# TensorE's order in two mixer branches, written out by a small planner instead of left to the scheduler

## The chip, the cores and the metric

The kernel runs on one core of a Trainium2 chip. The metric is the device time of one execution in microseconds (us), taken as the median of several runs. The engines in the rows are PE (TensorE, matmuls and transposes), DVE (VectorE), ACT (ScalarE), POOL (GpSimd), and SP, which here only issues DMAs.

## The reference

One decoder layer over 512 positions of width 1024, in float32. The part that matters:

```
h    = rmsnorm(x);  q,k,v,o,i,f | q,k,v | gates = split(h @ w_in)
A    = mlstm(silu(conv4(q)), silu(conv4(k)), v, i, f)          # 4 heads of 128
ya   = (sigmoid(o) * head_rmsnorm(A)) @ w_br_m
a    = softmax(q1 k1' / 8 + bias) - lam * softmax(q2 k2' / 8 + bias)   # 4 heads, causal
yb   = (head_rmsnorm(a @ v) * (1 - lam_init)) @ w_br_d
x    = x + (sigmoid(ga) * ya + sigmoid(gb) * yb) @ w_out
x    = x + convffn(rmsnorm(x));   x = x + gated embedding;   out = rmsnorm(x)
```

Only the lines down to `yb` are touched by the change.

## The kernel before

Everything lies transposed: features on the 128 partitions, the 512 positions along a row. A float32 value is split into a high part and the remainder (L90, `split`: an ACT copy, then a DVE subtraction), and a product is three matmuls into one PSUM tile (L98, `mm3`: high by high, low by high, high by low). A projection of 128 output features is eight such triples of 512 columns, 24 matmuls (L116, `proj`). Its weights come by a 512 KB DMA and are split by ACT (`whi`, 1.05 us) and DVE (`wlo`, 1.22 us), two buffers each.

PSUM has eight banks, given out by tag (L81): four "mm" for projections, two "acc" for sums over blocks (`num`, `den`, `av`), and two "sc" for all that is short: scores, transposed weights, column sums. The eight tiles `hm0ss` ... `hd3ss`, which hold a head's sum of squares, are "sc" tiles too, and `head_norm` keeps such a tile to the end of the inverse root: `rsqrt_of` writes its scratch `a` there, and L163 is the last reader.

The branch part, which starts when the first value projection is done, has these pieces:

- `mq`, `mk`: a projection, then four taps of a convolution and a tanh on DVE and ACT (L203). `dq`, `dk`, `dv`, `mo`, `ga`, `gb`: projections with short ends.
- mLSTM of a head (L427): for each of four blocks j a decay tile `rb` comes by DMA, ACT takes its exponent, POOL cuts the triangle, PE makes the scores `s`, DVE multiplies, ACT and DVE split the product into `pph`, `ppl`, and PE adds it into `num` and `den`. `rb` has three buffers.
- Attention of a head (L467): for each block of queries i and each half z two matmuls `ds`, a DVE pass that adds the bias and finds the maximum (L480), an ACT exponent; then PE transposes the weights into tiles `at` (L495), which ACT and DVE split into `aph`, `apl`, and PE adds them into `av`.
- `head_norm` (L410): y, the square, its split `csph`, `cspl`, two matmuls with ones into `hd0ss` and its kin, then a chain of ACT and DVE operations to `hdh`, `hdl`, the operands of the projections `yb` (for the mLSTM `hmh`, `hml` and `ya`).
- The merge (L552) makes `ya` and `yb` for eight output tiles, eight triples in all for each, with the gates still missing, and sums them; `wo` follows.

What sets the order: the list ORDER (L53) gives the order in which the pieces are recorded, and the scheduler then moves single instructions of each engine forward or back by its own estimate of when they are ready, among the constraints of buffers. So the small matmuls of a head come to stand between the matmuls of later projections. An engine carries out its own instructions in the order that results.

Of the kernel before, what the change touches and what calls it, by code (L numbers as in the profile page):

```python
# [16 lines left out]
P = 128  # L17
# [3 lines left out]
H = 4  # L21
# [29 lines left out]


ORDER = """  # L53
bias0 if0 mq0 mk0 mq1 mk1 ct0 m0 m1 mk3 mq2 dk0 M0 M1 mk2 m2 mq3 M2 m3 dq0 dv0 M3 a0 dk1 dq1
A0 a1 A1 dk2 dq2 ga3 dq3 a2 A2 ga0 ga2 gb1 dk3 a3 gb3 gb2 gb0 ga1 A3
"""


@with_exitstack
def trunk_kernel(ctx, tc, xT, pT, par, oneh, relb, lamv, w_if, w_in, w_v, w_br, w_out, w_up,  # L60
# [29 lines left out]
    def split(hi, lo, src, scale=None):  # L90
# [74 lines left out]
    def colsum(o, src):  # L165
        hi, lo = pair("cs")
        last = nc.scalar.copy(hi, src)
        nc.vector.tensor_sub(lo, src, f(hi))
        nc.tensor.matmul(o, lhsT=ones, rhs=hi, start=True, stop=False)
        nc.tensor.matmul(o, lhsT=ones, rhs=lo, start=False, stop=True)  # L170
        return last
# [95 lines left out]
    def vproj(i, name, first=None):  # L267
        os = [ps("mm", f"{name}p{b}") for b in range(NB)]
        xs = []
        for g in range(4):  # L270
            w = None if first else wload(w_v[4 * i + g])
            for kk in range(2):
                k = 2 * g + kk
                if first:
                    x = tt("x", f"x{k}")
                    nc.sync.dma_start(x, xT[:, k, :])
                    h.append(scaled(x, C_GMIX + k, f"h{k}"))
                    w = vw(i, g, kk, w)
                    if k == 1:
                        nc.sync.dma_start(prm[:, KD:], par[:, KD:])  # L280
                    xs.append(x)
                    if k:
                        sumsq_add(acc, xs[k - 1], k == 1)
                    if k == KD - 1:
                        sumsq_add(acc, x, False)
                        with tc.high_priority():
                            first()
                r = wk(w, kk, S)
                for b in range(NB):
                    a = [t[:, b * P:(b + 1) * P] for t in h[k]]  # L290
                    mm3(os[b], a, r, k == 0, k == KD - 1)
        vs = []
# [7 lines left out]
    def gates():  # L300
# [40 lines left out]
    def turn_cols(cols):  # L341
        o = ps("sc", "colp")
        for j in range(NB):
            nc.tensor.transpose(o[:, 4 * j:4 * j + 4], cols[:, j * P:(j + 1) * P], ident[0:H, 0:H])
        ct = cp.tile([P, NB * H], F32, name="ct")
        nc.vector.tensor_copy(ct, o[:, :NB * H])
        return ct


    def make_bias():  # L350
# [4 lines left out]
        for i in range(2):  # L355
# [3 lines left out]
            o = ps("acc", "bvp", 320)  # L359
            nc.tensor.matmul(o[0:H, :], lhsT=tab, rhs=oh, start=True, stop=True)  # L360
            bv = tt("hn", "bv", 320)[0:H, :]
# [32 lines left out]

    def weighted(name, j, src_parts, v, hh, outs):
# [6 lines left out]
        src_parts(ph[:, lead:], pl[:, lead:])  # L402
        o = outs[0][:, wide(j):]
        mm3(o, [t[:, hh * P:(hh + 1) * P] for t in v[j]], (ph, pl), j == 0, j == NB - 1)
        if len(outs) > 1:
            o = outs[1][:, wide(j):]
            nc.tensor.matmul(o, lhsT=ones, rhs=ph, start=j == 0, stop=False)
            nc.tensor.matmul(o, lhsT=ones, rhs=pl, start=False, stop=j == NB - 1)

    def head_norm(o, g, name, extra=None):  # L410
# [15 lines left out]

    def mlstm(hh):  # L427
        num, den = ps("acc", f"num{hh}"), ps("acc", f"den{hh}")
        for j in range(NB):
            n = S - j * P  # L430
            rb = tt("rb", "rb", n)
            nc.sync.dma_start(rb, rd[hh, ROW_OFF[j]:ROW_OFF[j + 1]].partition_broadcast(P))
            nc.scalar.activation(rb, rb, AF.Exp, bias=ct[:, j * H + hh:j * H + hh + 1])
            nc.gpsimd.affine_select(out=rb[:, 0:P], in_=rb[:, 0:P], pattern=[[1, P]],
                                    compare_op=ALU.is_ge, fill=0.0, base=0, channel_multiplier=-1)
            s = ps("sc", f"s{hh}{j}", S - wide(j))
            mm3(s, [t[:, j * P:(j + 1) * P] for t in mk[hh]], [t[:, wide(j):] for t in mq[hh]], True, True)
            nc.vector.tensor_mul(rb, s[:, j * P - wide(j):], rb)
            weighted("p", j, lambda a, b: split(a, b, rb), mv, hh, (num, den))
        return num, den  # L440

# [7 lines left out]

    def mlstm_end(hh, num, den, t):  # L450
        em = tt("rb", "em")
# [5 lines left out]
        nc.scalar.activation(em, em, AF.Square, scale=EPS ** 0.5)  # L457
        y = head_norm(num, C_GM + hh, f"hm{hh}", em)
        if t is None:
            t = out_gate(hh)  # L460
        nc.vector.scalar_tensor_tensor(y, t, 1.0, y, op0=ALU.add, op1=ALU.mult)
        hi, lo = rt("hz", f"hmh{hh}"), rt("hz", f"hml{hh}")
        split(hi, lo, y, 0.5)
        return hi, lo


    def attention(hh, q, k):  # L467
        av = []
        for i in range(NB):
            n = (i + 1) * P  # L470
            nw = max(n, 2 * P)
            es, sums = [], []
            for z in range(2):
# [15 lines left out]
            nc.vector.scalar_tensor_tensor(es[0], es[0], sums[0], es[1], op0=ALU.mult, op1=ALU.add)  # L489
            av.append(es[0])  # L490
        o = ps("acc", f"av{hh}")
        for j in range(NB):
            tps = ps("sc", f"at{hh}{j}", S - j * P)
            for i in range(j, NB):
                nc.tensor.transpose(tps[:, (i - j) * P:(i - j + 1) * P], av[i][:, j * P:(j + 1) * P], ident)  # L495
            weighted("a", j, lambda a, b: split(a, b, tps), dv, hh, (o,))
        return o

    def attention_end(hh, o):
        y = head_norm(o, C_GD + hh, f"hd{hh}")  # L500
        hi, lo = rt("hz", f"hdh{hh}"), rt("hz", f"hdl{hh}")
        split(hi, lo, y, 1.0 - LAM_INIT)
        return hi, lo

# [9 lines left out]
    mv = vproj(0, "mv", make_r)  # L514
    mq, mk, dq, dk, mo, sums, hm, hd, ga, gb = ({} for _ in range(10))
    for step in ORDER.split():
        what, i = step[:-1], int(step[-1])
        if what == "if":
# [7 lines left out]
        elif what == "mo":  # L526
            mo[i] = out_gate(i)
        elif what == "m":
            sums[i] = mlstm(i)
        elif what == "M":  # L530
            hm[i] = mlstm_end(i, *sums[i], mo.get(i))
        elif what == "dv":
            dv = vproj(1, "dv")
        elif what == "bias":
            bias, nlam = make_bias(), make_nlam()
        elif what == "dq":
            dq[i] = queries(8 + i, f"dq{i}")
# [247 lines left out]
```

## Time and profile before

| | us |
|---|---|
| median of 3 runs (lowest, highest) | 835.04 (834.36, 835.73) |
| the profiled execution, its own time | 833.08 |
| its span in the trace | 831.2 |
| PE busy | 809.1 (97%) |
| DVE, ACT busy | 552.4 (66%), 423.0 (51%) |
| branch part, first `if` matmul to first `wo` matmul | 31.48 to 356.21 |

The profiled execution takes 1.9 us more than its span, and 2.0 us less than the median. A row of a timeline gives the start, the duration and, in brackets, how long the engine stood idle before it and which engine's instruction it waited for. Durations of matmuls hold their latency; the spacing of starts is what PE can issue.

### The profile page before, as it was taken

Reading aid. Unit: us, or ns where it says so; the run is one execution under the profiler, and the core shown is the slowest. Engines: PE = TensorE matmul, PEld = TensorE weight load, DVE = VectorE, ACT = ScalarE, POOL = GpSimd, SP = SyncE. Lnnn points to the kernel's source line nnn. Section 1 sums busy time; section 2 is a strip of 40 time slices with the busy share of each in tenths; the row PEclk is TensorE's granted clock in tenths of the full one; section 3 lists DMA queues with packets and bytes.
Section 4 is the critical chain, followed back from the end, with each engine's and each line's share of the span. In section 5 each row is a group of like instructions: output and inputs, shape, how many; then the busy total and the mean of one; then the engine's idle time right before and its main releaser. Section 6 shows DMA issues by size and latency. Waiting matters only on the chain.

```text
span 831.2 us, 9840 instructions
## 1 busy us (share of the span) xinstructions
PE 809.1 (97%) x3635; PEld 661.5 (80%) x3635; DVE 552.4 (66%) x878; ACT 423.0 (51%) x627; POOL 24.7 (3%) x110
## 2 busy tenths in 40 slices
PE   8999999999999999999999999999999999999993
PEld 6777778887878888888788888888888888888882
DVE  7698787699867754455777777777777233343676
ACT  7456877787776433333644444444444332322653
POOL 0111101000000000000000000000000000000000
PEclk9999999999999999999999999999999999999997
DMA  7363333222122223343323322223222333333312
GB/s 223 119 212 108 102 109 112 76 77 76 52 78 74 94 89 98 139 165 102 105 98 102 102 101 92 89 99 102 102 101 82 91 106 103 89 95 95 101 52 101
DMA packets 29287, 85.43 MB, mean 103 GB/s; under 512 B 3430, under 2 KB 7162, under 8 KB 29112
## 3 DMA queue, kind: packets, MB, share of 16 engines
q1 hardware_dynamic: 28424, 82.22, 30.7%
q0 software_dynamic: 672, 2.59, 1.0%
q8 instruction: 28, 0.46, 0.2%
q14 instruction: 19, 0.16, 0.1%
q10 hardware_dynamic: 144, 0.00, 0.0%
HBM read 82.66 MB, written 3.45 MB: 104 GB/s over the span
## 4 chain that ended last, share of the span: by engine, by line
PE 79%; ACT 2%; DVE 2%; DMA 1%; issue 1%; DVEq 0%; ACTq 0%
PE uv L100 5%; PE wd L102 5%; PE wd L101 5%; PE uv L102 5%; PE uv L101 5%; PE wd L100 5%; PE ug L100 5%; PE ug L102 5%; PE ug L101 5%; PE gb L101 2%; PE gb L102 2%; PE gb L100 2%; PE ga L100 2%; PE ga L102 2%; PE ga L101 2%; PE wo L100 2%
## 5 line engine op out<-in xcount | busy, mean ns | idle before, releaser
L92 ACT CAST whi<-raw 128x1024 fp32r<-128x1024 f32 (+1 forms) x143 | 144.6, 1012 | 207.0 <-issue 73.7
L93 DVE TENSOR_TENSOR wlo<-raw,whi 128x1024 fp32r<-128x1024 f32 (+1 forms) x142 | 167.2, 1179 | 87.6 <-ACT whi L92 86.2
L100 PE MATMUL wd<-gh,whi 128*128 128x512 f32 x176 | 68.5, 389 | 0.0
L101 PE MATMUL wd<-gl,whi 128*128 128x512 f32 x176 | 68.5, 389 | 0.0
L102 PE MATMUL wd<-gh,wlo 128*128 128x512 f32 x176 | 68.5, 389 | 0.0
L591 DVE SCALAR_TENSOR_TENSOR y<-u,prm,y 128x512 f32<-128x512 f32 x88 | 65.6, 749 | 1.5
L92 ACT CAST gh<-y 128x512 fp32r<-128x512 f32 x22 | 13.7, 621 | 55.5 <-DVE y L600 55.5
L586 DVE TENSOR_TENSOR u<-uv,rffn 128x512 f32<-128x512 f32 x22 | 15.2, 692 | 38.2 <-PE uv L102 38.2
L100 PEld LDWEIGHTS wd<-gh,whi 128*128 128x128 f32 x176 | 33.0, 188 | 6.9
L101 PEld LDWEIGHTS wd<-gl,whi 128*128 128x128 f32 x176 | 33.0, 188 | 6.9
L102 PEld LDWEIGHTS wd<-gh,wlo 128*128 128x128 f32 x176 | 33.0, 188 | 6.7
L589 ACT ACTIVATE y<-u,prm 128x512 f32<-128x512 f32 x44 | 35.7, 814 | 0.2
L598 ACT ACTIVATE y<-y 128x512 f32<-128x512 f32 x22 | 13.9, 632 | 40.8 <-DVE y L591 40.8
L93 DVE TENSOR_TENSOR gl<-y,gh 128x512 fp32r<-128x512 f32 x22 | 15.2, 693 | 14.7 <-ACT gh L92 14.7
L100 PE MATMUL wo<-mxh,whi 128*128 128x512 f32 x64 | 24.9, 389 | 0.0
L101 PE MATMUL wo<-mxl,whi 128*128 128x512 f32 x64 | 24.9, 389 | 0.0
L102 PE MATMUL wo<-mxh,wlo 128*128 128x512 f32 x64 | 24.9, 389 | 0.0
L151 ACT ACTIVATE sq<-x 128x512 f32<-128x512 f32 x27 | 16.8, 621 | 9.3 <-DVE x L648 9.3
L484 ACT ACTIVATE e<-e,mx 128x128 f32<-128x128 f32 (+3 forms) x32 | 17.8, 558 | 7.1 <-DVE mx L483 6.8
L152 DVE TENSOR_TENSOR acc<-acc,sq 128x512 f32<-128x512 f32 x27 | 18.5, 686 | 3.0 <-ACT sq L151 3.0
L213 DVE SCALAR_TENSOR_TENSOR y<-u,prm,y 128x512 f32<-128x512 f32 x24 | 17.8, 743 | 2.1 <-ACT y L211 2.0
L574 DVE TENSOR_TENSOR x<-x,wo 128x512 f32<-128x512 f32 x8 | 5.5, 688 | 17.1 <-PE wo L102 17.1
(1063 smaller groups left out, 2202.9 us busy)
## 6 DMA issues: line engine op xcount, KB each, us to landing
raw<-in_w_up SPq DMA_DIRECT2D x44, 512.0 KB, 3.3
raw<-in_w_in SPq DMA_DIRECT2D x36, 512.0 KB, 3.4
raw<-in_w_down SPq DMA_DIRECT2D x16, 512.0 KB, 3.5
x<-in_xT SPq DMA_DIRECT2D x16, 256.0 KB, 4.4
raw<-in_w_br SPq DMA_DIRECT2D x8, 512.0 KB, 3.3
raw<-in_w_out SPq DMA_DIRECT2D x8, 512.0 KB, 3.6
raw<-in_w_gate SPq DMA_DIRECT2D x8, 512.0 KB, 3.3
raw<-in_w_down SPq DMA_DIRECT2D x8, 384.0 KB, 3.2
```

What stands on the lines that cost most here:

```text
L92: nc.scalar.copy(hi, src)
L93: nc.vector.tensor_sub(lo, src, f(hi))
L100: nc.tensor.matmul(o, lhsT=lh, rhs=rh, start=start, stop=False)
L101: nc.tensor.matmul(o, lhsT=lh, rhs=rl, start=False, stop=False)
L102: nc.tensor.matmul(o, lhsT=ll, rhs=rh, start=False, stop=stop)
L151: nc.scalar.activation(q, src, AF.Square)
L152: nc.vector.tensor_add(acc, acc, q)
L213: nc.vector.scalar_tensor_tensor(y, u[:, i:i + S], col(c0 + i), y, op0=ALU.mult, op1=ALU.add)
L484: nc.scalar.activation(e, e, AF.Exp, bias=mx[:, 1:2], accum_out=mx[:, 2:3])
L586: nc.vector.tensor_mul(u[:, 2:514], o, rB)
L589: nc.scalar.activation(y, u[:, 2:514], AF.Identity, scale=col(c0 + 2), bias=col(c0 + 3))
L591: nc.vector.scalar_tensor_tensor(y, u[:, i:i + S], col(c0 + i), y, op0=ALU.mult, op1=ALU.add)
```

## The change

The instructions of PE between the value projection and the end of the branch part are marked to stay in the order in which they are recorded (`mmul`, `turn`, `placed`, as long as `kept` holds). That order is made while recording: `clock` counts the columns of the matmuls recorded so far, at (n + 32) / 2400 us for each. A new list gives the projections; the heads' small products are generators that give back the clock at which they want to go on, after fixed lags (`LAG_S` behind scores, `LAG_CS` between a head's square and its column sum, ...), and `poll`, called ahead of every triple of a projection, runs those that are due. Scores of the mLSTM are made one and two blocks ahead; a head of the attention begins before the values of the head before it are made. `queries` of heads 1 to 3 take tiles of another tag. The arithmetic, the tiles of each tag and all other stages are as before; the merge loop itself is recorded with `kept` off, so its matmuls are placed by the scheduler among the fixed ones.

```diff
-bias0 if0 mq0 mk0 mq1 mk1 ct0 m0 m1 mk3 mq2 dk0 M0 M1 mk2 m2 mq3 M2 m3 dq0 dv0 M3 a0 dk1 dq1
-A0 a1 A1 dk2 dq2 ga3 dq3 a2 A2 ga0 ga2 gb1 dk3 a3 gb3 gb2 gb0 ga1 A3
+if0 mq0 mk0 bias0 mo0 mq1 mk1 ct0 ga0 mq2 gb0 mk2 mo1 mq3 ga1 mk3 mo2 dq0 dk0 dv0 dk1 dq1 mo3 dk2 dq2 gb1
+ga2 dk3 dq3 gb2 ga3 gb3
 """
+LAG_CONV, LAG_COLS, LAG_HALVES = 10.0, 4.0, 6.0
+LAG_S, LAG_DS, LAG_E, LAG_AT, LAG_V, LAG_CS = 5.5, 3.0, 7.0, 4.0, 4.0, 6.0
...
+    def placed(ins, n):
+        nonlocal clock
+        if kept:
+            tc.keep_in_program_order(ins)
+            clock += (n + 32) / 2400
+
+    def mmul(o, l, r, start, stop):
+        placed(nc.tensor.matmul(o, lhsT=l, rhs=r, start=start, stop=stop), r.shape[-1])
...
+    def poll():
+
+        while True:
+            t = next((t for t in tasks if t[0] <= clock), None)
+            if t is None:
+                return
+            try:
+                t[0] = next(t[1])
+            except StopIteration:
+                tasks.remove(t)
...
     def proj(o, w, k0, acts, start=True, stop=True):
         n = len(acts)
         for i, a in enumerate(acts):
+            poll()
             mm3(o, wk(w, k0 + i), a, start and i == 0, stop and i == n - 1)
...
+        hi, lo = pair("cs")
+        last = nc.scalar.copy(hi, v)
+        nc.vector.tensor_sub(lo, v, f(hi))
+        yield clock + LAG_CS
         ss = ps("sc", name + "ss")
-        last = colsum(ss, v)
+        mmul(ss, ones, hi, True, False)
+        mmul(ss, ones, lo, False, True)
...
+            p = [scores(0), scores(1)]
+            for j in range(NB):
+                yield p[j][1] + LAG_S
+                weighted(j, p[j][0], mv, hh, (num, den))
+                if j + 2 < NB:
+                    p.append(scores(j + 2))
...
+            if i < NB - 1:
+                yield clock + LAG_DS
+        free(6 if hh == 0 else 4)
+        tasks.append([clock + LAG_E, values(hh, av)])
+        if hh + 1 < H:
+            tasks.append([clock, attention(hh + 1)])
...
+        a = [turn_block(0), turn_block(1)]
+        o = ps("acc", f"av{hh}")
         for j in range(NB):
+            yield a[j][1] + LAG_AT
+            weighted(j, a[j][0], dv, hh, (o,))
+            if j + 2 < NB:
+                a.append(turn_block(j + 2))
+        told.append(hh)
+        tasks.append([clock, attention_end(hh, o)])
...
+    while steps or tasks:
+        poll()
+        for what, i in steps:
+            n = need.get(what, 0) if (what, i) not in (("dq", 1), ("dq", 2), ("dq", 3)) else 0
+            if live + n <= QK and (what != "mo" or i == 0 or i - 1 in hm) and (n or what != "dq" or "m" in done):
+                steps.remove((what, i))
...
+                project(what, i)
+                done[f"{what}{i}"] = clock
+                break
+        else:
+            if tasks:
+                log.append((round(clock, 1), "wait"))
+                clock = max(clock + 0.1, min(t[0] for t in tasks))
+    kept = False
```

Three places of PE's order follow, each before and after. In names as `ds110` the digits are head, block of queries and half; in `at10` they are head and block of keys. First PE before, where the scores of head 1 stand between the projections `dk2` and `dq2`:

```order
L100 MATMUL dk2_1990<-h7h_282,whi_1992 128x512
L101 MATMUL dk2_1990<-h7l_283,whi_1992 128x512
L476 MATMUL ds110_1861<-dk1h0_1766,dq10_1811 128x256
L476 MATMUL ds110_1861<-dk1l0_1767,dq10_1811 128x256
L102 MATMUL dk2_1990<-h7h_282,wlo_1993 128x512
L100 MATMUL dq2_2035<-h0h_106,whi_2037 128x512
L101 MATMUL dq2_2035<-h0l_107,whi_2037 128x512
L476 MATMUL ds111_1870<-dk1h1_1772,dq11_1814 128x256
L476 MATMUL ds111_1870<-dk1l1_1773,dq11_1814 128x256
L102 MATMUL dq2_2035<-h0h_106,wlo_2038 128x512
L100 MATMUL dq2_2035<-h1h_130,whi_2037 128x512
```

and the same scores now, from the sum of squares of head 0 on:

```order
L112 MATMUL hd0ss_1963<-csph_1897,ones_89 128x512
L112 MATMUL hd0ss_1963<-cspl_1898,ones_89 128x512
L112 MATMUL dk2_1947<-h3h_180,whi_1949 128x512
L112 MATMUL dk2_1947<-h3l_181,whi_1949 128x512
L112 MATMUL dk2_1947<-h3h_180,wlo_1950 128x512
L112 MATMUL ds110_1982<-dk1h0_1802,dq10_1868 128x256
L112 MATMUL ds110_1982<-dk1l0_1803,dq10_1868 128x256
L112 MATMUL ds111_1991<-dk1h1_1808,dq11_1871 128x256
L112 MATMUL ds111_1991<-dk1l1_1809,dq11_1871 128x256
L112 MATMUL dk2_1947<-h4h_204,whi_1949 128x512
L112 MATMUL dk2_1947<-h4l_205,whi_1949 128x512
```

Before, `ds111` stood four matmuls behind `ds110`; now it follows it at once, and both follow `hd0ss` more closely.

Next, PE before, around the first scores of head 2:

```order
L102 MATMUL ga_2296<-h2h_153,wlo_2299 128x512
L169 MATMUL hd1ss_1970<-csph_1971,ones_89 128x512
L476 MATMUL ds200_2147<-dk2h0_2023,dq20_2068 128x256
L476 MATMUL ds200_2147<-dk2l0_2024,dq20_2068 128x256
L100 MATMUL ga_2296<-h3h_180,whi_2298 128x512
L101 MATMUL ga_2296<-h3l_181,whi_2298 128x512
L102 MATMUL ga_2296<-h3h_180,wlo_2299 128x512
L100 MATMUL ga_2296<-h4h_204,whi_2298 128x512
L170 MATMUL hd1ss_1970<-cspl_1972,ones_89 128x512
L476 MATMUL ds201_2156<-dk2h1_2029,dq21_2071 128x256
```

and now, from the transposes of head 1 on:

```order
L115 MATMUL at10_2151<-ident_94,e0_2041 128x128
L115 MATMUL at10_2151<-ident_94,e0_2076 128x128
L115 MATMUL at11_2160<-ident_94,e0_1985 128x128
L115 MATMUL at11_2160<-ident_94,e0_2041 128x128
L115 MATMUL at11_2160<-ident_94,e0_2076 128x128
L112 MATMUL ds200_2169<-dk2h0_2016,dq20_2101 128x256
L112 MATMUL ds200_2169<-dk2l0_2017,dq20_2101 128x256
L112 MATMUL ds201_2178<-dk2h1_2022,dq21_2104 128x256
L112 MATMUL ds201_2178<-dk2l1_2023,dq21_2104 128x256
L112 MATMUL ga_2141<-h1h_130,whi_2143 128x512
```

Before, the first scores of head 2 stood alone between matmuls of `ga`; now they follow seven transposes into the two tiles `at10` and `at11` with nothing between.

Last, PE before, at the end of the last head (`hdh3` is what comes of `hd3ss`; the line of dots stands for 21 more matmuls of `ya` and `yb` that don't use it):

```order
L170 MATMUL hd3ss_2708<-cspl_2710,ones_89 128x512
L100 MATMUL ya_2734<-hmh2_1283,whi_2729 128x512
L101 MATMUL ya_2734<-hml2_1284,whi_2729 128x512
L102 MATMUL ya_2734<-hmh2_1283,wlo_2730 128x512
L100 MATMUL ya_2734<-hmh3_1604,whi_2729 128x512
...
L101 MATMUL ya_2773<-hml3_1605,whi_2768 128x512
L102 MATMUL ya_2773<-hmh3_1604,wlo_2769 128x512
L100 MATMUL yb_2774<-hdh0_1837,whi_2768 128x512
L100 MATMUL yb_2735<-hdh3_2724,whi_2729 128x512
```

and now:

```order
L112 MATMUL yb_2774<-hdh2_2623,whi_2768 128x512
L112 MATMUL yb_2774<-hdl2_2624,whi_2768 128x512
L112 MATMUL yb_2774<-hdh2_2623,wlo_2769 128x512
L112 MATMUL hd3ss_2712<-csph_2708,ones_89 128x512
L112 MATMUL hd3ss_2712<-cspl_2709,ones_89 128x512
L112 MATMUL yb_2735<-hdh3_2724,whi_2729 128x512
L112 MATMUL yb_2735<-hdl3_2725,whi_2729 128x512
L112 MATMUL yb_2735<-hdh3_2724,wlo_2730 128x512
L112 MATMUL yb_2774<-hdh3_2724,whi_2768 128x512
```

Before, 28 matmuls of the merge stood between `hd3ss` and the first product with `hdh3`; now there is none, and the products of `yb` with heads 0 to 2 stand ahead of `hd3ss`.

## Rows read from the trace of the kernel before

**Rows 1.** The page: span, and engines with busy time, share of the span, instructions.

```profile
span 831.2 us, 9840 instructions
PE 809.1 (97%) x3635; PEld 661.5 (80%) x3635; DVE 552.4 (66%) x878; ACT 423.0 (51%) x627; POOL 24.7 (3%) x110
```

**Rows 2.** Windows: length, busy time (x instructions) of PE, PEld, DVE, ACT, POOL; PEclk.

```profile
31.48:356.21 324.73, 320.21 (x1471) 259.17 (x1471) 240.41 (x464) 199.49 (x332) 18.15 (x60) 1.00 0.32 102
440.00:460.00 20.00, 20.00 (x90) 16.57 (x89) 14.55 (x18) 8.34 (x11) 0.40 (x4) 1.00 0.31 101
820.00:831.00 11.00, 0.00 (x0) 0.00 (x0) 7.23 (x20) 1.22 (x3) 0.00 (x0) 0.51 0.54 191
```

**Rows 3.** Waits of PE: what ended each; us in total, times, longest.

```profile
PE num L100 <- ACT pph L92: 2.3, 4, 1.1
PE s L100 <- ACT mk0h L95: 1.8, 1, 1.8
```

**Rows 4.** Timeline of PE: start, us, instruction, [idle before it <- releaser].

```profile
1.52 3.65 PE L129 MATMUL warm<-idle 128*128 128x512 f32 x9 [1.52 <-DVE idle L126]
61.59 0.39 PE L102 MATMUL mk<-h4h,wlo 128*128 128x512 f32 x1
61.82 0.39 PE L100 MATMUL mk<-h5h,whi 128*128 128x512 f32 x1
63.96 0.50 PE L100 MATMUL s<-mq0h,mk0h 128*128 128x512 f32 x1 [1.75 <-ACT mk0h L95]
64.30 0.40 PE L101 MATMUL s<-mq0l,mk0h 128*128 128x512 f32 x1
```

**Rows 5.** Timeline: two transposes of attention weights, then the copies out of their banks.

```profile
177.86 0.38 PE L495 MATMUL at<-ident,e 128*128 128x128 f32 x2
178.22 0.97 ACT L92 CAST aph<-at 128x512 fp32r<-128x512 f32 x2
178.92 1.16 DVE L93 TENSOR_TENSOR apl<-at,aph 128x512 fp32r<-128x512 f32 x2
```

**Rows 6.** Timeline: the last score matmul of a bank, then its reader.

```profile
187.97 0.28 PE L476 MATMUL ds<-dk1l,dq 128*128 128x256 f32 x1
188.29 0.43 DVE L480 CUSTOM_DVE_ANT_0 e<-ds,bias 128x256 f32<-128x256 f32 x1 [0.49 <-PE ds L476]
```

**Rows 7.** Timeline: hd0ss's second matmul, and the last reader of its bank.

```profile
186.20 0.42 PE L170 MATMUL hd0ss<-cspl,ones 128*128 128x512 f32 x1
192.04 0.69 DVE L163 SCALAR_TENSOR_TENSOR r<-hd0ss,r 128x512 f32<-128x512 f32 x1
```

**Rows 8.** DMA issues, and lines by form: the decay tiles of 256 columns.

```profile
rb<-rd SPq DMA_DIRECT2D x2, 128.0 KB, 2.9
L433 ACT ACTIVATE rb<-rb,ct 128x256 f32<-128x256 f32 x4 | 2.0, 508 | 1.4 <-DMA raw<-in_w_in 0.8 <-DMA rb<-rd 0.5
L434 POOL TENSOR_SCALAR_AFFINE_SELECT rb<-rb 128x128 f32<-128x128 f32 x14 | 4.7, 341 | 45.4 <-ACT rb L433 32.3 <-DMA rb<-rd 5.7 <-DVE em L456 5.0
L438 DVE TENSOR_TENSOR rb<-s,rb 128x256 f32<-128x256 f32 x4 | 1.7, 417 | 0.0
```

**Rows 9.** Timeline: the last head's end.

```profile
266.42 0.28 PE L102 MATMUL av<-aph,dvl 128*128 128x256 f32 x1
267.94 0.62 ACT L167 CAST csph<-v 128x512 fp32r<-128x512 f32 x1
269.88 0.40 PE L170 MATMUL hd3ss<-cspl,ones 128*128 128x512 f32 x1
270.69 0.68 DVE L419 TENSOR_SCALAR v<-hd3ss 128x512 f32<-128x512 f32 x1
275.65 0.63 ACT L95 ACTIVATE hdh<-y 128x512 fp32r<-128x512 f32 x1 [2.21 <-DVE y L424]
277.86 0.42 PE L101 MATMUL yb<-hdl,whi 128*128 128x512 f32 x1
278.32 1.05 ACT L92 CAST whi<-raw 128x1024 fp32r<-128x1024 f32 x1 [2.04 <-PE yb L101]
```

More of the change, by code (lines that the diff above doesn't have):

```diff
@@ L168, in colsum @@
         nc.vector.tensor_sub(lo, src, f(hi))
-        nc.tensor.matmul(o, lhsT=ones, rhs=hi, start=True, stop=False)
-        nc.tensor.matmul(o, lhsT=ones, rhs=lo, start=False, stop=True)
+        mmul(o, ones, hi, True, False)
+        mmul(o, ones, lo, False, True)
         return last
@@ L359, in make_bias @@
             o = ps("acc", "bvp", 320)
[L360 removed]
+            mmul(o[0:H, :], tab, oh, True, True)
             bv = tt("hn", "bv", 320)[0:H, :]
@@ L401, in weighted @@
             nc.gpsimd.memset(f(pl[:, :lead]), 0.0)
[L402 to L408, printed above, removed]
+        split(ph[:, lead:], pl[:, lead:], src)
+        return ph, pl
+    def weighted(j, p, v, hh, outs):
+        mm3(outs[0][:, wide(j):], [t[:, hh * P:(hh + 1) * P] for t in v[j]], p, j == 0, j == NB - 1)
+        for o in outs[1:]:
+            o = o[:, wide(j):]
+            mmul(o, ones, p[0], j == 0, False)
+            mmul(o, ones, p[1], False, j == NB - 1)
     def head_norm(o, g, name, extra=None):
@@ L425, in head_norm, with mlstm, scores @@
         return y
[L427 to L440, printed above, removed]
+    def mlstm():
+        for hh in range(H):
+            while f"mk{hh}" not in done or f"mq{hh}" not in done or "ct0" not in done:
+                yield clock + 0.1
+            yield max(done[f"mk{hh}"] + LAG_CONV, done[f"mq{hh}"] + LAG_CONV, done["ct0"] + LAG_COLS)
+            num, den = ps("acc", f"num{hh}"), ps("acc", f"den{hh}")
+            def scores(j):
+                rb = tt("rb", "rb", S - j * P)
+                nc.sync.dma_start(rb, rd[hh, ROW_OFF[j]:ROW_OFF[j + 1]].partition_broadcast(P))
+                nc.scalar.activation(rb, rb, AF.Exp, bias=ct[:, j * H + hh:j * H + hh + 1])
+                nc.gpsimd.affine_select(out=rb[:, 0:P], in_=rb[:, 0:P], pattern=[[1, P]],
+                                        compare_op=ALU.is_ge, fill=0.0, base=0, channel_multiplier=-1)
+                s = ps("sc", f"s{hh}{j}", S - wide(j))
+                mm3(s, [t[:, j * P:(j + 1) * P] for t in mk[hh]], [t[:, wide(j):] for t in mq[hh]], True, True)
+                nc.vector.tensor_mul(rb, s[:, j * P - wide(j):], rb)
+                return parts("p", j, rb), clock
+            p = [scores(0), scores(1)]
[4 more added lines that the diff above has]
+                    p.append(scores(j + 2))
+                    if j + 2 == NB - 1:
+                        free(4)
+            tasks.append([clock, mlstm_end(hh, num, den)])
+            if hh == H - 2:
+                tasks.append([clock, attention(0)])
+            yield clock + 0.1
+        done["m"] = clock
@@ L457, in mlstm_end, with attention @@
         nc.scalar.activation(em, em, AF.Square, scale=EPS ** 0.5)
[L458 to L461, printed above, removed]
+        y = yield from head_norm(num, C_GM + hh, f"hm{hh}", em)
+        while hh not in mo:
+            yield clock + 0.1
+        nc.vector.scalar_tensor_tensor(y, mo[hh], 1.0, y, op0=ALU.add, op1=ALU.mult)
         hi, lo = rt("hz", f"hmh{hh}"), rt("hz", f"hml{hh}")
         split(hi, lo, y, 0.5)
-        return hi, lo
-    def attention(hh, q, k):
+        hm[hh] = (hi, lo)
+    turned = [0] * H
+    def attention(hh):
+        while f"dk{hh}" not in done or f"dq{hh}" not in done:
+            yield clock + 0.1
+        yield max(done[f"dk{hh}"], done[f"dq{hh}"]) + LAG_HALVES
+        q, k = dq[hh], dk[hh]
         av = []
         for i in range(NB):
+            while hh and turned[hh - 1] <= i:
+                yield clock + 0.1
             n = (i + 1) * P
@@ L490, in attention, with values, turn_block @@
             av.append(es[0])
+            if i < NB - 1:
[4 more added lines that the diff above has]
+            tasks.append([clock, attention(hh + 1)])
+    def values(hh, av):
+        while "dv0" not in done or "m" not in done or hh != len(told):
+            yield clock + 0.1
+        yield done["dv0"] + LAG_V
+        def turn_block(j):
+            tps = ps("sc", f"at{hh}{j}", S - j * P)
+            for i in range(j, NB):
+                turn(tps[:, (i - j) * P:(i - j + 1) * P], av[i][:, j * P:(j + 1) * P], ident)
+            turned[hh] += 1
+            return parts("a", j, tps), clock
+        a = [turn_block(0), turn_block(1)]
         o = ps("acc", f"av{hh}")
         for j in range(NB):
[L493 to L497, printed above, removed]
+            yield a[j][1] + LAG_AT
[4 more added lines that the diff above has]
+        tasks.append([clock, attention_end(hh, o)])
     def attention_end(hh, o):
-        y = head_norm(o, C_GD + hh, f"hd{hh}")
+        y = yield from head_norm(o, C_GD + hh, f"hd{hh}")
         hi, lo = rt("hz", f"hdh{hh}"), rt("hz", f"hdl{hh}")
         split(hi, lo, y, 1.0 - LAM_INIT)
-        return hi, lo
+        hd[hh] = (hi, lo)
     def gate(c, name):
@@ L514, in trunk_kernel, with free, project @@
     mv = vproj(0, "mv", make_r)
-    mq, mk, dq, dk, mo, sums, hm, hd, ga, gb = ({} for _ in range(10))
-    for step in ORDER.split():
-        what, i = step[:-1], int(step[-1])
+    mq, mk, dq, dk, mo, hm, hd, ga, gb, done = ({} for _ in range(10))
+    live, told = 0, []
+    def free(n):
+        nonlocal live
+        live -= n
+    def project(what, i):
+        nonlocal rd, cols, ct, dv, bias, nlam
         if what == "if":
```

44 lines of the change are left out of this document (24 added, 20 removed).

## Prediction

> **What bounds the kernel now.** I read the page first: PE is busy for 97% of the span, DVE for 66%, ACT for 51% [rows 1]. Then the windows: in the stretch from 440 to 460, far behind the branches, 90 matmuls fill 20.00 us with no idle time at a granted clock of 1.00, the level of 2.4 GHz; that is the pace of 512 columns, which the timeline has as 0.23 us from start to start [rows 2, 4]. The branch part is the only stage where PE waits at all, and little: from 31.48 to 356.21 it is busy for 320.21 of 324.73 us, so 4.5 us idle [rows 2]. The list of waits names most of that: four waits of `num` for `pph`, 2.3 us, and one of `s` for `mk0h`, 1.8 us [rows 3]; two more of 0.2 us make up the rest. A wait costs a little more than its idle time. Between the last `mk` matmul and the `s` that waited, starts lie 2.14 us apart and the next 0.34 us, where 0.23 is usual: 2.0 us lost for 1.75 us idle [rows 4]. So an order without any wait would gain about 4.5 + 5 x 0.27 = 5.9 us here, and nothing elsewhere: the matmuls and their columns are the same.
>
> The question is therefore which waits the new order brings. PE issues in the order written, so a matmul that waits for a bank or an operand holds all that stand behind it, ready projections too. I went through the new order piece by piece with durations from the rows. Times below are delays of PE's next start.
>
> **The end of the last head.** Before, the last `av` matmul starts at 266.42 and the high part of the square, `csph`, is done at 268.56, 2.14 us later. Now seven matmuls of `yb` stand between, 1.6 us, so the first `hd3ss` matmul is held some 0.4 us, and the second 0.45 more, since `cspl` (0.7 us on DVE) follows `csph`. Then comes the chain. Before, the second matmul of `hd3ss` starts at 269.88, and `hdh` is done at 276.28; 0.4 us of that is a wait of L419 for DVE, which was at other work, so the chain takes 6.0 us [rows 9]. It was free, as 28 matmuls of the merge covered it (28 x 0.227 = 6.4 us). Now a product with `hdh3` stands at once behind `hd3ss`: 6.0 less the matmul's own slot of 0.23 is 5.8 us of waiting. The second product needs `hdl3`, one DVE pass of 0.7 us later, less a slot: 0.45. Six products on, the merge needs the third weight block; its `whi` takes a buffer that those products read last. Before, ACT began such a copy 0.46 us behind the releasing matmul and took 1.05 [rows 9]; five slots cover 1.1 of 1.5 us, so 0.4 stays. Sum: 0.4 + 0.45 + 5.8 + 0.45 + 0.4 = 7.5 us. Bounds: 6.5 (the operations of the chain without gaps, 5.5, and the least of the rest) and 8.5 (ACT or DVE busy once, about one weight pass).
>
> **Two halves of a score in one bank.** `hd0ss` holds one of the two "sc" banks from 186.20 to 192.73, 6.5 us [rows 7]. Where one is held, `ds110` and `ds111` share the other, and they now stand back to back. A score bank is free when its DVE pass has ended, 0.75 us after its last matmul's start [rows 6]; less that matmul's slot of 0.12 this is 0.63, and 0.75 for three blocks with their longer pass. By the same count `ds020` and `ds021` meet in one bank. Together 1.4 us, from 1.2 to 2.8 (DVE late by one pass). Before, three matmuls or more lay between such halves.
>
> **Held banks that are wanted again.** From `hd0ss` to `ds121`, which wants its bank, the order has 18 matmuls of 0.227 us and six short ones, 4.9 us, and with the waits above some 5.7, against the 6.5 held. I take 0.7 here, and 0.3 where `at21` wants the bank of `hd1ss`: 1.0 in all. Below, 0 if the chain is quicker than in the row; above, 5.2, as ACT stands in each chain behind whatever is ready, and two more table loads stand in its order.
>
> **Transposes with scores behind them.** Now `ds200` takes the bank of `at10` with only the three transposes of `at11` between. The trace shows two transposes from 177.86; the first ACT copy begins at 178.22, and DVE's first pass at 178.92, to end at about 179.6 [rows 5]. From the last transpose at 178.00 that is 1.6 us; three transposes cover 0.35 and the slot 0.1, so 1.15. `ds201` needs `at11`, whose pass ends 0.45 later, less 0.2: 1.4 us for the pair. Three more places have smaller tiles (`at13` and `ds210`; `ds300` behind head 2's; head 3's own): 0.5, 0.6, 0.8. Sum 3.3, from 2.8 to 4.4. On this the Trainium skill, "Perfetto Trace Analysis", section "Optimizing Tensor Performance", says that independent groups should rotate through banks so that the copy out of one overlaps the next group's matmuls. Here two banks do rotate, and by that rule alone this term would be zero; the rows say that a copy takes 1.6 us and the next group 0.35, so I stay with 3.3.
>
> **mLSTM.** In heads 1 to 3 the sum of squares of the head before holds one bank, so `s13` must wait until DVE has multiplied `s12`. Its decay tile can only be fetched when a buffer of `rb` is free, by the order about when `num1` begins: 2.9 us to land, 0.51 for the exponent, 0.34 on POOL, 0.42 for the product [rows 8], 4.2 us; the matmuls of `num1`, `den1` and `s12` cover 2.4. That is 1.8 us. The first scores of heads 2 and 3 stand 10 us behind their convolution, whose ACT and DVE operations are over 6 us and queue with others; I take 1.0 for both. Sum 2.8, from 0 (tiles earlier, lag enough) to 4.6.
>
> **After each wait** the next start is 0.11 late [rows 4]; some 13 waits make 1.4 us, from 1.0 to 1.8. Weight loads, DMAs and the queue of SP carry the same transfers and stay ahead by the buffers; I cost them at nothing, since projections of 5.4 us cover a DMA and both splits of a block; were one late, it would cost about one split, 1.1 us. The two table loads are in ACT's half-free time, and enter by the bound above.
>
> **Sum.** 7.5 + 1.4 + 1.0 + 3.3 + 2.8 + 1.4 = 17.4 us new, less 5.9 removed: +11.5 us. The profiled execution, 833.1 us, would become 844.6; on the median, 835.0, which is 2.0 higher, that is 846.5. The low ends give 6.5 + 1.2 + 0 + 2.8 + 0 + 1.0 - 5.9 = +5.6, so 840.6; the high ends 8.5 + 2.8 + 5.2 + 4.4 + 4.6 + 1.8 - 5.9 = +21.4, so 856.4. The likeliest case's own range is 841 to 855.
>
> **Rivals.**
> A, faster: the order does away with the old waits and its own stay under 5.9 us. One mechanism would do it: the scheduler's matmuls of the merge come to cover half of the hd3 chain and the lags hide the banks. Then 3.8 us of the end stay, less 5.9: -2.1, so 832.9. For it: ACT and DVE have a third and a half of their time free. Against it: the order shows no matmul between `hd3ss` and the product with `hdh3`, and 5.5 us of operations can't run side by side. It decides at 5.9 us of new waiting.
> B, the end alone: the lags are long enough everywhere in the middle, and only the end (6.5 to 7.5) and a few bank waits (1.2) are left: 6.5 + 1.2 + 0.5 - 5.9 = +2.3, so 837.3. For it: the lags (5.5, 3, 4 us) are longer than most chains in the rows. Against it: the order puts scores straight behind transposes, where no lag counts.
> C, the clock: behind a wait of some 6 us PE might come back at its lower level. In the rows the granted clock is 1.00 through the branches and 0.51 once PE has stopped at the end [rows 2]; the nine first matmuls of the program took 406 ns each [rows 4]. Nine such at the merge would add 9 x 0.18 = 1.6 us, so 848.1, and more if other waits do it too. For and against: the longest wait in the branches, 1.75 us, is followed by matmuls at the usual spacing, but it is three times shorter. The Trainium skill, "TensorE: Matmul & The Clock Gate", section "Why this matters for your kernels", says that idle gaps between bursts bring the lower clock; it is this rival's mechanism, and no row of this trace has a gap of such a length ahead of further work.
>
> **Chances.** Forecast 0.55; C, which shares its mechanism, 0.15; B 0.17; A 0.08; no change, where the new waits happen to equal the old, 0.05. About 0.2% can be told from no change. Faster 0.08, same 0.05, slower 0.87. The range, 836 to 856 us, leaves out A, the case of no change and the far end of the bounds.
>
> **What would show it.** In the trace after: PE idle ahead of the first `yb` with `hdh` for 5 to 6 us, ended by ACT, with `whi` of the next block soon behind; `num` and `s` waits mostly gone in head 0; waits of `ds` for ACT or DVE behind `at`, and of `s` for DVE; from `wo` on the same spacing as before, shifted. The branch part would be 11 to 12 us longer. I am wrong if PE's idle time in that part is below 6 us, or if the part is shorter than 324.7 us; the size is wrong if the end is right and the rest is near zero.

## The result, and the profile after

The changed kernel is slower: 861.48 us (median of 4, 860.84 to 862.89) against 835.36 for the kernel before in the same runs, a ratio of 1.0331 with an interval of 1.0317 to 1.0346. The forecast had the sign, but 846.5 us, and the time lies outside its range. The profiled execution took 862.89 us, the highest of the four, and is compared with the profiled one of before at 833.08; that pair differs by 29.8 us, the medians by 26.1.

The page of the kernel after, beside [rows 1]; the third line is the granted clock of PE in 40 slices:

```profile
span 861.1 us, 9833 instructions
PE 818.5 (95%) x3635; PEld 670.4 (78%) x3635; DVE 557.8 (65%) x878; ACT 426.6 (50%) x629; POOL 26.6 (3%) x110
PEclk9999999999998989999999999999999999999997
```

Windows of it, with the columns of [rows 2]: the branch part, five stretches in it, and a stretch far behind it.

```profile
30.94:386.21 355.27, 329.64 (x1473) 267.55 (x1473) 246.46 (x465) 203.76 (x334) 20.04 (x59) 0.97 0.29 93
99.50:102.50 3.00, 3.00 (x9) 2.41 (x9) 1.86 (x6) 1.03 (x2) 0.08 (x2) 0.50 0.25 87
147.50:150.40 2.90, 2.90 (x8) 2.34 (x8) 2.64 (x5) 2.43 (x4) 0.00 (x0) 0.50 0.00 0
259.50:263.00 3.50, 3.50 (x11) 2.72 (x10) 2.68 (x5) 1.11 (x2) 0.10 (x1) 0.53 0.09 35
269.50:273.00 3.50, 3.50 (x12) 2.78 (x11) 1.75 (x10) 0.88 (x4) 0.00 (x0) 0.56 0.22 88
306.90:310.90 4.00, 4.00 (x10) 3.06 (x10) 2.74 (x4) 2.32 (x3) 0.00 (x0) 0.50 0.00 0
440.00:460.00 20.00, 20.00 (x90) 16.57 (x89) 17.36 (x24) 11.68 (x14) 0.40 (x4) 1.00 0.29 101
```

The branch part is 355.27 us long, 30.5 more than before, and from `wo` on the pace is the old one. Two numbers of the first row split the loss: PE is idle for 25.6 us, where it was 4.5, and busy for 329.6 us, where it was 320.2, with the same matmuls. The five stretches that follow say what the second part is: PE is busy all the time, at a granted clock of about 0.50, the level of 1.2 GHz. Summed over all matmuls there that start some 0.43 us apart instead of 0.23, these stretches cost 1.6, 1.5, 1.7, 1.5 and 2.5 us, 8.8 us in all. So of the 30.5 us, 21.1 are waiting and 8.8 clock; 0.6 us is left over.

The waits of PE after, beside [rows 3] (the largest; the columns are those of there):

```profile
PE yb L112 <- ACT hdh L99: 5.7, 1, 5.7
PE ds L112 <- DVE apl L97: 3.8, 3, 2.0
PE ds L112 <- DVE r L194: 3.1, 1, 3.1
PE at L115 <- DVE r L194: 2.8, 1, 2.8
PE s L112 <- DVE rb L482: 2.2, 2, 1.8
PE ds L112 <- DVE mx L545: 2.1, 2, 1.5
PE s L112 <- ACT mk3h L99: 1.3, 1, 1.3
PE s L112 <- DVE ct L378: 1.2, 1, 1.2
PE mk L112 <- ACT whi L96: 0.8, 1, 0.8
PE mk L112 <- DVE wlo L97: 0.7, 1, 0.7
```

The waits of `num` and of `s` for `mk0h` are gone, as the order was to do; in their place stand the ten reasons above and a few smaller ones. Most of them are DVE's: a bank that it hasn't read yet (`apl`, `r`, `rb`, `mx`, `ct`).

### The profile page after: what moved, and what is told of

It reads as the page before. It is cut to its first block, busy times and chain, and to the rows that moved or that the text cites. A ratio compares the mean times of both kernels' runs of the same rounds, so it can differ in the third digit from the quotient of the medians.

```text
span 861.1 us, 9833 instructions
## 1 busy us (share of the span) xinstructions
PE 818.5 (95%) x3635; PEld 670.4 (78%) x3635; DVE 557.8 (65%) x878; ACT 426.6 (50%) x629; POOL 26.6 (3%) x110
## 4 chain that ended last, share of the span: by engine, by line
PE 78%; DVE 9%; ACT 6%; DMA 3%; issue 3%; SPq 0%; DVEq 0%; POOL 0%; ACTq 0%; POOLq 0%
PE wd L112 14%; PE uv L112 14%; PE ug L112 13%; PE wo L112 5%; PE pg L112 4%; PE ga L112 4%; PE gb L112 4%; PE ya L112 3%; PE yb L112 3%; PE dvp L112 2%; DVE wlo L97 2%; PE dk L112 2%; PE dq L112 1%; ACT whi L96 1%; PE pw L112 1%
## 5 line engine op out<-in xcount | busy, mean ns | idle before, releaser
L698 DVE SCALAR_TENSOR_TENSOR y<-u,prm,y 128x512 f32<-128x512 f32 x88 | 65.6, 748 | 1.5
L112 PE MATMUL yb<-hdh,whi 128*128 128x512 f32 x32 | 13.5, 421 | 5.7 <-ACT hdh L99 5.7
L545 DVE CUSTOM_DVE_ANT_0 e<-ds,bias 128x128 f32<-128x128 f32 (+3 forms) x32 | 15.1, 486 | 5.6 <-PE ds L112 5.5
```

The source lines that it names most:

```text
L112: placed(nc.tensor.matmul(o, lhsT=l, rhs=r, start=start, stop=stop), r.shape[-1])
L545: nc.vector.tensor_tensor_reduce(out=e, in0=s[:, :n], in1=bias[hh][:, S - n:], scale=0.125, scalar=-3.0e38, op0=ALU.add, op1=ALU.max, accu ...
L698: nc.vector.scalar_tensor_tensor(y, u[:, i:i + S], col(c0 + i), y, op0=ALU.mult, op1=ALU.add)
```

## The experiments

The theory, from the profile after: the order has PE wait for banks and operands that come later than the lags say, no ready projection can step in, and PE's idling brings the lower clock on top. What is open is whether the list, the marking, the banks or the end makes the waits, and whether the slow stretches are due to idling at all.

**The marking taken away**, the recording kept (`e1_free`):

```diff
         if kept:
-            tc.keep_in_program_order(ins)
             clock += (n + 32) / 2400
```

> Theory A (the cost lies in the order in which the pieces are recorded: waits for banks and for the hd3 chain, and a lower clock behind them; marking it as fixed adds little): with the marking taken away and the recording kept, the time stays within 4 us of the changed kernel, 858 to 865 us, with the 5.7 us wait ahead of the first product with hdh3 still there. Theory B (the marking itself is the cost, as the scheduler may no longer fill a wait with ready projections): the time falls back to 835 to 845 us and the waits of ds, at and s for DVE are gone.

Measured: 840.45 us, ratio 1.0078 (1.0052 to 1.0105). The time is the one that theory B gave; theory A had the end right and the middle wrong. The marking is the greater part of the loss, 21 us of it. The largest waits of this kernel, whose lines are numbered one lower:

```profile
PE yb L111 <- ACT hdh L99: 5.7, 1, 5.7
PE at L114 <- DVE r L193: 0.9, 1, 0.9
PE num L111 <- ACT pph L96: 0.9, 1, 0.9
```

and its branch part:

```profile
31.25:363.65 332.40, 322.75 (x1473) 261.25 (x1473) 244.46 (x466) 208.25 (x338) 18.35 (x59) 0.99 0.31 100
```

PE is idle for 9.7 us, and 5.7 of that is the one wait at the end. The two orders differ in some thirty places, mostly by a few steps. Between a small product and the one that stood directly ahead of it now lie 5 matmuls of `mk2` at `s13`, 7 of `dk2` at `ds111`, 4 of `dq2` at `ds121`, 8 of `gb` at `at21`, 9 of `ga` at `ds300` and 12 of `ga` at `ds200`, projections that were ready. Such steps are the cover that the marking forbade.

**Half of the marking**, up to the end of mLSTM (`g1_half_marked`):

```diff
-            tc.keep_in_program_order(ins)
+            if "m" not in done:
+                tc.keep_in_program_order(ins)
```

> The changed kernel's recording, with the order of PE marked as fixed only until the last head of mLSTM is done. Theory A (the marking costs wherever a bank or an operand is late, in both branches apart): the changed kernel reaches the second value projection 8.1 us after e1_free (157.76 against 149.68 in the traces) and the column sum of head 3 another 14 us after it; so half the marking costs 8 us, 847 to 850 us, and the waits of ds and at for r, apl and mx that were 12 us are gone. Rival (the attention part of the cost is a consequence of the late mLSTM part): the time stays above 855 us or falls to within 3 us of e1_free.

Measured: 847.28 us, ratio 1.0159 (1.0135 to 1.0183), 6.8 us over the kernel without marking; `ds` and `at` waited 1.3 us in all. That is theory A's: the cost arises in both branches, one third in mLSTM.

**The bank given back early**, with the marking (`e2_bank`) and without (`f4_free_bank`):

```diff
-        rsqrt_of(r, v, ss, last)
+        rsqrt_of(r, v, tt("hn", "a"), last)
```

> The scratch of the heads' inverse root lies in SBUF, so that the bank of a head's sum of squares comes free after one DVE pass instead of some 6.5 us. Theory A (held banks): the waits ds for r (3.12 us), at for r (2.85) and s for rb in head 1 (1.75) go, and with two of them the slow matmuls that follow (1.6 and 1.7 us); with 0.27 us around each wait that is 11 to 12 us, 849 to 852 us. Rival (two banks are too few whoever holds them: the next group waits for the same bank soon after): at most 3 us, 858 us or more.

Measured: 855.10 us, ratio 1.0246 (1.0214 to 1.0277). The gain is 6.4 us, between the two theories. The waits for `r` are gone, and others have grown, `ds` for `mx` from 2.1 to 3.7 us and `s` for `mk2` from 0.6 to 2.6:

```profile
PE ds L112 <- DVE mx L545: 3.7, 1, 3.7
PE ds L112 <- DVE apl L97: 3.3, 3, 1.6
PE s L112 <- ACT mk2h L99: 2.6, 1, 2.6
```

> e1_free with the scratch of e2_bank in SBUF. Theory A (once small products may be moved, a held bank costs next to nothing): 839 to 841 us, against 840.5 for e1_free. Rival (banks still decide): 835 to 837 us, as much as the 6.4 us that the same edit gave with the marking.

Measured, without the marking: 839.48 us, ratio 1.0062 (1.0047 to 1.0077), 1.0 us less than `e1_free`; the intervals of the two ratios overlap, so this difference can't be told from none. As theory A had it: the held banks cost 6 us net where the order is fixed, and some 1 us or nothing where a small product may step back.

**Products that only fill.** Their result is read by nobody. In the first kernel (`e3_fill`) they stand at six places, in the second (`h1_fill4`) at four of these, without the groups of 11 ahead of `ds121` and of 22 behind `hd3ss`. The edit, and one of the places:

```diff
+    def fill(n):
+        d = ps("mm", "dum")
+        for i in range(n):
+            tc.keep_in_program_order(nc.tensor.matmul(d, lhsT=ones, rhs=h[0][0], start=i == 0, stop=i == n - 1))
...
+                if (hh, j) in ((1, 3), (3, 0)):
+                    fill(5 if hh == 1 else 4)
```

> 27 products more than are needed, written to a bank that nobody reads, stand ahead of four matmuls that waited long (s13, ds121, at21, the first ds of head 3 and, with 22 more, behind hd3ss), each group a little shorter than the wait that it fills; nothing that is needed changes. Theory A (the 0.43 us spacing behind waits is the lower level of PE's clock, brought by its idling): the waits stay as delays, but the five stretches at 0.43 us are gone or nearly, 8.8 us in all less what lies behind the wait of s30, which isn't all filled: 6 to 9 us less, 852.5 to 855.5 us, granted clock 1.00 all along. Rival (the matmuls behind a wait are slow for reasons of their own, as operands that have just been written): no gain, 860 to 863 us, or a loss where a group is longer than its wait.

Measured: 865.07 us, ratio 1.0369 (1.0343 to 1.0395): a loss. The middle went as theory A says: the granted clock is 1.00 from 30 to 263, and the first `ds` of head 3, at 269.01 in the changed kernel, starts at 264.41, though 36 products more stand ahead of it. But the 22 products at the end drew the merge's matmuls behind themselves, so that head 3's transposes waited 4.2 us for weights with nothing to do, and the first half of the fillers ran at the low clock themselves (0.53 from 285 to 299). The test was spoilt by its own end, hence the second. (The expectation miscounts the products: there are 5, 4, 11, 10 and 6 in the middle, 36, and 22 at the end.)

> The changed kernel with 25 products more, written to a bank that nobody reads: 5 ahead of s13, 4 ahead of s30, 10 ahead of at21 and 6 ahead of the first ds of head 3, each group shorter than the wait it fills (in all 5.7 us of 8.0 us); the order of all else is that of the changed kernel, the end of the last head too. Theory A (PE's idling brings the lower clock, and that is some 9 us of the loss): the waits stay, and the four slow stretches behind them (1.6, 1.5, 1.7 and 1.5 us) go: 855 to 858 us for more work, and the stretch behind the wait for hdh3 stays. Rival (products behind a wait are slow for another reason): 861 to 864 us, with the stretches still there.

Measured: 858.86 us, ratio 1.0302 (1.0282 to 1.0323), 2.6 us less than the changed kernel though PE does 5.7 us more work; all four runs lie below the changed kernel's lowest. Windows around the four filled places, then around two that were left:

```profile
99.50:102.50 3.00, 3.00 (x15) 2.55 (x16) 2.97 (x7) 2.10 (x5) 0.32 (x3) 1.00 0.21 73
144.50:150.40 5.90, 5.54 (x25) 4.59 (x25) 5.87 (x10) 2.51 (x4) 0.54 (x1) 1.00 0.04 6
257.80:261.40 3.60, 3.60 (x18) 3.03 (x19) 2.90 (x5) 1.11 (x2) 0.10 (x1) 1.00 0.13 49
266.00:270.00 4.00, 4.00 (x20) 3.41 (x21) 1.80 (x11) 0.88 (x4) 0.00 (x0) 1.00 0.29 111
214.20:218.00 3.80, 3.80 (x11) 3.07 (x12) 3.74 (x10) 0.78 (x2) 0.00 (x0) 0.59 0.44 138
301.60:306.50 4.90, 4.90 (x11) 3.52 (x12) 3.59 (x5) 2.62 (x3) 0.00 (x0) 0.50 0.03 8
```

All four slow stretches are gone where PE was kept at work, and the one at the end stands, as theory A had it. A new one appears behind `ds121`, whose wait of 3.1 us was there before without such an effect: 1.5 us of the 6.3 are given back so, and `wo` comes 4.3 us earlier than in the changed kernel's trace. That PE's idling brings the low clock is shown; which wait does it varies, and why it varies is not shown.

**The end.** `gb0` behind `dq3`, `dk3` and `dq3` ahead of `ga2`, `LAG_E` 4, first with the marking (`e4_tail`), then without (`f1_free_tail`):

```diff
-if0 ... ct0 ga0 mq2 gb0 mk2 mo1 ... dk2 dq2 gb1
-ga2 dk3 dq3 gb2 ga3 gb3
+if0 ... ct0 ga0 mq2 mk2 mo1 ... dk2 dq2 gb1
+dk3 dq3 gb0 ga2 gb2 ga3 gb3
```

> In the list gb0 stands behind dq3 instead of between mq2 and mk2, dk3 and dq3 come before ga2, and LAG_E is 4 instead of 7, so that head 3 is done earlier and 26 matmuls of the merge are left to stand behind hd3ss. Theory A (the wait for hdh3 is the lack of cover): that wait, 5.7 us, and the slow stretch behind it, 2.5 us, shrink to under 1 us together; up to 2 us come back at s20, which loses gb0 ahead of it: 853 to 857 us. Rival (the cover is only moved: the middle then lacks it, and a shorter LAG_E makes at wait for the weights): 859 to 863 us.

Measured: 867.62 us, ratio 1.0405 (1.0379 to 1.0431). The wait for `hdh3` is gone, as the cover says, but mLSTM lost more than it gave; neither theory had that much:

```profile
PE s L112 <- DVE rb L482: 13.1, 3, 7.5
PE at L115 <- DVE e L554: 4.8, 3, 2.0
```

> The list and lag of e4_tail (gb0 behind dq3, dk3 and dq3 ahead of ga2, LAG_E 4) without the marking. Theory A (what the marking costs is that a small product can't be moved by a few matmuls when its bank is late, and what is left without it is only the uncovered end): the wait for hdh3 is gone as in e4_tail and the middle waits stay near e1_free's 5 us: 831 to 836 us. Rival (without gb0 the decay tiles of mLSTM are late whoever orders, as s waited 13.1 us in e4_tail): s or num wait 5 us and more, 838 to 846 us.

Measured: 833.04 us, ratio 0.9986 (0.9976 to 0.9995). The same list and lags, 34.6 us faster for want of the marking; `s` waits 1.5 us instead of 13.1.

**Lists and lags without the marking.** `f2_mo_late`, with `LAG_E` 4 besides:

```diff
-mo3 dk2 dq2 gb1
-ga2 dk3 dq3 gb2 ga3 gb3
+dk2 dq2
+dk3 dq3 mo3 gb1 ga2 gb2 ga3 gb3
```

and `f3_short_lags`:

```diff
-ga2 dk3 dq3 gb2 ga3 gb3
+dk3 dq3 ga2 gb2 ga3 gb3
 ...
-LAG_S, LAG_DS, LAG_E, LAG_AT, LAG_V, LAG_CS = 5.5, 3.0, 7.0, 4.0, 4.0, 6.0
+LAG_S, LAG_DS, LAG_E, LAG_AT, LAG_V, LAG_CS = 5.5, 2.0, 3.0, 3.0, 4.0, 4.0
```

> Without the marking, gb0 left in its place; dk3, dq3, then mo3 and the gates behind dq2, LAG_E 4, so that 19 matmuls of the merge (4.3 us) are left behind hd3ss. Theory A: of e1_free's 840.5 us the end gives back some 5 us, with the clock behind it: 833 to 837 us, wait for hdh3 1 to 2 us. Rival (cover is taken from the heads before, which wait instead): 838 us or more.

Measured: 832.53 us, ratio 0.9979 (0.9969 to 0.9988), a little below theory A's range, with 1.5 us of waiting for `hdh3`.

> Without the marking; dk3 and dq3 ahead of ga2 and the lags of the attention shorter (LAG_DS 2, LAG_E 3, LAG_AT 3, LAG_CS 4), so that 18 matmuls (4.1 us) stand behind hd3ss. Theory A: 833 to 837 us with a wait for hdh3 of 1 to 2 us. Rival (the short lags bring waits of ds and at that the scheduler doesn't see): 838 us or more, with 3 us or more of waits of ds, at and av.

Measured: 831.75 us, ratio 0.9974 (0.9962 to 0.9986), again below theory A's range. It has the lowest median here; `f1_free_tail`, `f2_mo_late` and it all lie below the kernel before, by 0.1 to 0.3%, and their intervals overlap, so they aren't told apart. Its branch part:

```profile
31.00:355.61 324.61, 320.45 (x1472) 259.65 (x1472) 243.14 (x465) 199.37 (x332) 18.61 (x59) 1.00 0.32 102
```

and its largest waits:

```profile
PE yb L111 <- ACT hdh L99: 1.6, 1, 1.6
PE num L111 <- ACT pph L96: 0.9, 1, 0.9
PE s L111 <- DVE rb L481: 0.7, 1, 0.7
```

PE is idle for 4.2 us, 0.4 less than in [rows 2]: with PE at work for 97% of the span, there was little to win.

`f3_short_lags` with `ga1` behind `dq3`:

```diff
-mq3 ga1 mk3 ... dk3 dq3 ga2 gb2 ga3 gb3
+mq3 mk3 ... dk3 dq3 ga1 ga2 gb2 ga3 gb3
```

> f3_short_lags with ga1 moved from between mq3 and mk3 to behind dq3, so that 42 matmuls of the merge (9.5 us) stand behind hd3ss instead of 18. Theory A: the last 1.6 us of waiting for hdh3 and 0.4 for whi go, and at s30 without ga1 up to 1 us comes back: 830 to 832 us. Rival (without ga1 the first scores of head 3 or the decay tiles are late): 833 us or more.

Measured: 834.07 us, ratio 1.0000 (0.9986 to 1.0013): the rival. `s` waits 2.0 us for `rb`, and `hdh3` is still waited for, 1.5 us, behind 9.5 us of cover, since the chain has grown. ACT's table loads in it, behind the end of `csph`:

```profile
266.13 1.28 ACT L188 ACT_TABLE_LOAD   x1
268.49 1.28 ACT L595 ACT_TABLE_LOAD   x1
270.43 1.28 ACT L189 ACT_TABLE_LOAD   x1
272.38 1.28 ACT L190 ACT_TABLE_LOAD   x1
```

A gate's tanh (L595) slipped in behind the table that had been loaded ahead for the chain, and three more loads followed: the tanh's own, one for the logarithm and one for the exponent. `hdh` is done at 278.35, 11.4 us after the second matmul of `hd3ss` at 266.97, instead of the 6.4 of [rows 9].

The fastest list, that of `f3_short_lags`, with the marking put back (`g2_marked_best`):

```diff
         if kept:
+            tc.keep_in_program_order(ins)
             clock += (n + 32) / 2400
```

> The list and the lags of f3_short_lags, 831.8 us, with the order of PE marked as fixed. Theory A (the marking costs whatever the list, since lags are counted in PE's columns and know nothing of banks and of DVE's queue): 850 to 858 us, with waits of s for rb and of ds and at for DVE as in the changed kernel, without the one for hdh3. Rival (it was the list of the changed kernel that didn't suit the marking): 832 to 840 us.

Measured: 862.95 us, ratio 1.0347 (1.0312 to 1.0382), 31 us more than without. The waits are others than in the changed kernel:

```profile
PE at L115 <- DVE e L554: 11.6, 3, 4.5
PE hm1ss L112 <- ACT csph L452: 2.4, 1, 2.4
```

Theory A holds and its number was too low: none of the three lists that were run with the marking suits it.

## Why the prediction failed in size

The way of working was borne out: each kind of wait that it named is in the trace. By its own steps, in us of PE's idle time (the forecast's 1.4 us behind the waits left out, as the idle time doesn't hold them):

| step | forecast | measured |
|---|---|---|
| end of the last head | 7.5 | 6.2 (0.3 + 0.2 + 5.7) |
| two halves of a score in one bank | 1.4 | 2.1 (0.7 + 1.5) |
| held banks that are wanted again | 1.0 | 6.0 (3.1 + 2.85) |
| transposes with scores behind them | 3.3 | 3.7 (1.4 + 0.3 + 2.0) |
| mLSTM | 2.8 | 4.5 (1.75 + 0.5 + 0.6 + 1.3 + 0.4) |
| weights (`mk` 1.6), the bank of the gates' columns (`ct` 1.2), `at` for `e` (0.3), costed at nothing | 0 | 3.1 |
| sum | 16.0 | 25.6 |
| clock, forecast as rival C | 1.6 | 8.8 |

The removed 4.5 us of idle time went as forecast. The profiled pair differs by 29.8 us where 11.5 were forecast. The 18.3 us that were missed are the clock (8.8, of which the sum had nothing), the held banks (5.0), what was costed at nothing (3.1), mLSTM (1.7) and the halves and transposes (1.1), less 1.3 at the end. So two steps failed above all. Of what was costed at nothing, the weights of `mk1` should have been covered by a projection of 5.4 us; ACT began their `whi` at 57.77, with operations of a convolution ahead of it, and PE was ready for them at 58.05 (in `e1_free` the same copy began at 55.85, and PE didn't wait).

**Held banks.** The step put 6.5 us, the length of the chain in [rows 7], against 5.7 us of cover. The chain of `hd0ss` after, from its second matmul to its last reader, and who waited:

```profile
206.94 0.39 PE L112 MATMUL hd0ss<-cspl,ones 128*128 128x512 f32 x1
208.55 1.28 ACT L190 ACT_TABLE_LOAD   x1
209.84 0.63 ACT L190 ACTIVATE r<-v 128x512 f32<-128x512 f32 x1
210.49 1.28 ACT L549 ACT_TABLE_LOAD   x1
212.30 0.71 ACT L191 ACTIVATE r<-r,lnb 128x512 f32<-128x512 f32 x1
214.66 0.69 DVE L193 SCALAR_TENSOR_TENSOR hd0ss<-v,hd0ss 128x512 f32<-128x512 f32 x1
215.26 1.22 DVE L97 TENSOR_TENSOR wlo<-raw,whi 128x1024 fp32r<-128x1024 f32 x1
216.39 0.68 DVE L194 SCALAR_TENSOR_TENSOR r<-hd0ss,r 128x512 f32<-128x512 f32 x1
217.13 0.44 PE L112 MATMUL ds<-dk1h,dq 128*128 128x384 f32 x1 [3.12 <-DVE r L194]
```

It takes 10.1 us, not 6.5. Two table loads stand in it, 1.28 us each, one ahead of the logarithm and one, for an exponent of the attention, between the logarithm and the chain's own exponent; and a weight pass of DVE stands ahead of the last operation. The chain of `hd1ss`, whose bank `at21` waited 2.85 us for:

```profile
250.17 0.39 PE L112 MATMUL hd1ss<-cspl,ones 128*128 128x512 f32 x1
258.41 0.69 DVE L194 SCALAR_TENSOR_TENSOR r<-hd1ss,r 128x512 f32<-128x512 f32 x1
```

It takes 8.9 us without any table load: exponents of the attention and splits of weights on ACT and DVE stand between its operations. I had seen the bound (5.2 us of waiting, less than the 6.0 that came) and took a value near the row of before instead; a chain over two busy engines has no fixed length, and the cover of 5.7 us was set against the shortest case. The experiment with the early bank shows the step's weight under the marking, 6.4 us net of the waits that grew, and without it some 1.0, which can't be told from none.

**The clock.** Rival C stood for one stretch at the end. The trace has five, behind waits of 1.3 to 5.7 us, and the kernels with filling products show that the idling brings them. The row I leaned on, a wait of 1.75 us in [rows 4] with no slow matmul behind it, was one case taken for a rule. The Trainium skill, "TensorE: Matmul & The Clock Gate", section "Why this matters for your kernels", which I cited for C, says that idle gaps between bursts bring the lower clock; the trace agrees, with 8.8 us, and has it behind shorter waits too than the gap that the page warns of. I weighed it at one wait of many.

The rule on rotating through banks from the Trainium skill, "Perfetto Trace Analysis", section "Optimizing Tensor Performance", would have had the transposes free; the trace has 3.7 us there, beside the 3.3 worked out from the copies' durations.

Rivals A and B fell: A's condition, less than 5.9 us of new waits, is missed by 20; of B, the end alone, only `e1_free` is an instance (840.45, where B had 837.3 for it), which is what the change would have been without the marking. That the waits come from the marking rather than from the list I had not asked: the forecast took the order as given and never compared it with what the scheduler makes of the same list.

What stays open is why the two profiled executions differ by 3.7 us more than the medians. That of before lies 2.3 us under its median and that of after 1.4 over its own. The slow stretches may lie behind other waits in other executions, as `h1_fill4` suggests, but no second profile of the changed kernel shows it.

## What to carry to other kernels

Where an engine is near full, a fixed order costs its waits in full: each small product must stand behind the slowest case of what it needs, not the usual one, or be free to step back behind ready work. A list with lags is good as a hint (831.75 us) and bad as a law (862.95 us, the same list). Count for every wait that a new order brings what the clock may take behind it (1.5 to 2.5 us here, at five of nineteen waits), and ask of every long chain at the end of a stage what stands behind it on the engine that waits.

## What the hardware showed that I had not expected

PE's granted clock fell to 0.50 behind waits as short as 1.3 us (`s30`, with a second of 0.4 us a microsecond later) and 1.75 us (`s13`), and the matmuls then started 0.43 us apart for 3 to 4.7 us:

```profile
306.18 0.79 PE L112 MATMUL yb<-hdh,whi 128*128 128x512 f32 x1 [5.67 <-ACT hdh L99]
307.50 0.63 PE L112 MATMUL yb<-hdh,wlo 128*128 128x512 f32 x1
307.92 0.63 PE L112 MATMUL yb<-hdh,whi 128*128 128x512 f32 x1
```

A wait of 3.12 us at `ds121` brought nothing in one execution and 1.5 us in another with the same order there.
